# Adaptive-norm modulations: products on ScalarE, sums on GpSimd, in a two-block kernel on one core

## The chip, the core and the metric

One core of a Trainium2 chip runs the whole kernel. The core has five engines with queues of their own, each of which runs its instructions in order: TensorE (PE, its weight loads are shown as PEld), VectorE (DVE), ScalarE (ACT), GpSimd (POOL) and SyncE (SP). SP issues most DMAs, GpSimd some. Engines wait for one another by semaphores. The metric is the device time of one execution in microseconds (us). Before the change it is 1889.6 us, the median of 3 runs (1889.45 to 1890.53).

## What is computed

Two transformer-like blocks on a sequence of 512 tokens and width 1024, all in float32. The first mixes with RWKV-7 and mLSTM heads and has a mixture of 32 experts, the second mixes with a 31-tap convolution and Mamba-2 heads and has a dense feed-forward part. Each block modulates its norms and residuals with vectors that come from a condition `c`:

```
mod = jax.nn.silu(c) @ ada_w[l] + ada_b[l]
sh_m, sc_m, g_m, sh_f, sc_f, g_f = jnp.split(mod, 6, axis=-1)
h = modulate(rms_norm(x, mix_norm_w[l]), sh_m, sc_m)
...
x = x + g_m[:, None, :] * y
```

The second block has the same with two matrices of three parts each. So there are twelve vectors of 1024, each a product of a vector of 1024 with a 1024x1024 matrix (4 MB). Two of the twelve, the first block's shift and scale of its first norm, are made by a function of their own at the start; the change concerns the other ten.

## The kernel before

Weights come from HBM through SP as raw blocks of 128 partitions x 1024 floats (`wload`, L189, three raw buffers). `wcut` splits each: ScalarE copies a high part in TensorE's rounded format (`whi`, L201), VectorE subtracts it to get the low part (`wlo`, L203). There are two buffers of each. TensorE then does three matmuls per product (high times high, high times low, low times high). One such block is consumed in about 24 matmuls of 128x512.

The program is written as straight Python and ordered before it runs: a planner walks all instructions with priorities and modelled times and fixes the order of every engine's queue; the semaphore waits follow from the data. A tile's buffer is handed on when its last reader is done. Work that is not urgent is written as generators: `K.later(gen, q)` puts one into a list, `K.pump(n, q)` runs the next n of its steps, each at a priority that is lowered by `LATER[q]` (600 places for list 0), so that such a step fills gaps. `K.drain(q)` runs what is left.

A modulation is such a generator. `ada_acc` (L261 on) takes an accumulator `acc` of 128x1024 from the tag `v4` and loads the matrix in eight pieces `araw` of 128x1024 (512 KB, SP, L269), each in a buffer of `v4` as well. Partition p of piece q holds row 128q+p. VectorE multiplies the first piece by a column of silu(c) (L273) and for each of the other seven does one multiply-add into `acc` (L275). Then `ada_cols` (L281 on) sums over the partitions with eight matmuls against a column of ones (L289) and adds the bias (L290); `ada_row` (L299 on) does it with ones as weights (L311), adds the bias and stores the row to DRAM from GpSimd's queue (L317).

`v4` has five buffers in the first mixer, four in the second, five in the last part. The same tag serves others: in the first mixer `solve` (L627 on) holds three for A, T and Ttmp while it inverts triangular 32x32 blocks on VectorE, `halves` takes Dm (cleared on GpSimd, L664, filled by two transposes on VectorE, L666, read by TensorE for pX) and X (L674); `scan` takes two. In the second mixer the decays E use it.

Where the ten run: gate_m, scale_f and shift_f, gate_f, scale_m2 and shift_m2 are pumped in the first mixer, under `RWKV.project`, `MLSTM.project` and `scan`. The scan is a chain over 32 units in which TensorE, ScalarE (R1, SA, StP, s1) and VectorE (the state, masks, copies) alternate; beside it runs the mLSTM `mix` generator with four powers on GpSimd (L1086), each followed by scalings on ScalarE (L1088). gate_m2, scale_f2 and shift_f2 are pumped in the second mixer beside the out-projection of the SSM part (`ssm_out`, pso), the last of the 31-tap convolution on VectorE (`conv31`, co L1996) and its layer norm: `conv_sums` (mean by TensorE, L2025; differences L2029; squares on ScalarE L2034; sum L2037; a power on GpSimd L2017; `spread` by TensorE) and `conv_norm` (L2053, L2054). In the same stretch `conv_out` makes eight gates (sgc, a ScalarE activation that frees a PSUM tile, L2068). gate_f2 is pumped in the feed-forward part.

GpSimd computes little: fills, selects, the powers of rsqrt. Its queue also issues DMAs (spills, fetches, stores).

Of the kernel before, what the change touches and what calls it, by code (L numbers as in the profile page):

```python
# [11 lines left out]
AF = mybir.ActivationFunctionType  # L12
ALU = mybir.AluOpType
# [9 lines left out]
class Kern:  # L23
# [237 lines left out]
    def ada_acc(self, cs, w, n0, width=1024):  # L261

        nc = self.nc
        V = nc.vector
        acc = self.v4([128, 1024], name="acc") if width == 1024 else self.u(name="acc")
        nq = 1024 // width
        for q0 in range(0, 8, nq):
            raw = self.v4([128, nq, width], name="araw")
            nc.sync.dma_start(raw, w[q0 * 128:(q0 + nq) * 128, n0:n0 + width].rearrange("(q p) n -> p q n", p=128))  # L269
            for i in range(nq):  # L270
                q = q0 + i
                if q == 0:
                    V.tensor_scalar(acc, raw[:, i], cs[:, 0:1], None, op0=ALU.mult)  # L273
                else:
                    V.scalar_tensor_tensor(acc, raw[:, i], cs[:, q:q + 1], acc, op0=ALU.mult, op1=ALU.add)  # L275
            yield acc

        for _ in range(self.SLACK):
            yield acc
# [2216 lines left out]
```

## Time and profile before

| | |
|---|---|
| median of 3 runs | 1889.6 us |
| profiled execution, its own time | 1887.34 us |
| its span (first to last instruction) | 1885.6 us |
| TensorE busy | 1779.2 us (94%) |
| VectorE busy | 1369.6 us (73%) |
| ScalarE busy | 943.3 us (50%) |
| GpSimd busy | 137.0 us (7%) |
| mean granted TensorE clock | 0.978 |
| L275, the multiply-adds | 70, 89.7 us |

All durations of the trace are from the one profiled execution. A row of a group of instructions gives the line of the kernel, the engine, the operation, what it writes and reads by tile name, and the shapes. Busy time counts an instruction from its start to its end; two neighbours can overlap by some tens of nanoseconds. Idle time stands in brackets or at the end of a row, with what ended it, as far as the semaphores tell. The granted clock is a share of the full 2.4 GHz, averaged over the stretch; the lower level is 1.2 GHz.

### The profile page before, as it was taken

The numbers are of one execution on the slowest core, as the hardware profiler recorded it, in microseconds if no ns is written. First come the engines' busy times: TensorE is split into PE (matmuls) and PEld (weight loads), VectorE is DVE, ScalarE is ACT, GpSimd is POOL, SyncE is SP. The second block draws the span as 40 slices with busy tenths as digits, with TensorE's granted clock in tenths as the row PEclk, the third lists the DMA queues.
The fourth block names the chain that finished last, engine by engine and source line by source line (L and its number), as shares of the span: only waits on it lengthen the run. The fifth ranks groups of instructions, "written<-read, shape, count | busy, mean of one in ns | idle before, by whom it ended". The sixth has DMA issues, their size and how long they took to land. (4 is left out here: it accounts for less than half of the span.)

```text
span 1885.6 us, 27902 instructions
## 1 busy us (share of the span) xinstructions
PE 1779.2 (94%) x10696; PEld 1481.2 (79%) x10696; DVE 1369.6 (73%) x2166; ACT 943.3 (50%) x1568; POOL 137.0 (7%) x247
## 2 busy tenths in 40 slices
PE   6998989998999998699999999999999999999997
PEld 3675878887888887478887777878778988788997
DVE  4888877867899997678969999999766753333324
ACT  5732355455888887442348577552253632223223
POOL 4000020121000000220000000000000100000000
PEclk9998989998999998899999999999999999999999
DMA  8732555535899999854433243344834753333334
GB/s 287 255 103 76 150 171 176 177 135 179 275 354 351 360 363 317 283 73 125 123 90 101 79 124 95 96 133 134 230 94 151 237 183 90 101 101 90 118 108 150
DMA packets 332905, 322.27 MB, mean 171 GB/s; under 512 B 16813, under 2 KB 291791, under 8 KB 332764
## 3 DMA queue, kind: packets, MB, share of 16 engines
q1 hardware_dynamic: 319004, 281.96, 47.7%
q0 software_dynamic: 11520, 35.30, 6.4%
q10 hardware_dynamic: 2240, 3.15, 0.5%
q8 instruction: 86, 1.41, 0.3%
q14 instruction: 55, 0.45, 0.1%
HBM read 299.03 MB, written 21.33 MB: 170 GB/s over the span
## 5 line engine op out<-in xcount | busy, mean ns | idle before, releaser
L201 ACT ACTIVATE whi<-wraw 128x1024 fp32r<-128x1024 f32 (+1 forms) x281 | 293.5, 1045 | 618.9 <-PE pin L237 209.8
L203 DVE TENSOR_TENSOR wlo<-wraw,whi 128x1024 fp32r<-128x1024 f32 (+1 forms) x281 | 337.9, 1203 | 210.9 <-ACT whi L201 208.5
L236 PE MATMUL pin<-hhi,whi 128*128 128x512 f32 (+1 forms) x752 | 306.4, 407 | 10.7 <-ACT sgc L2068 4.9
L238 PE MATMUL pin<-hhi,wlo 128*128 128x512 f32 (+1 forms) x752 | 300.3, 400 | 1.7 <-DVE wlo L203 1.7
L237 PE MATMUL pin<-hlo,whi 128*128 128x512 f32 (+1 forms) x752 | 300.7, 400 | 0.0
L236 PEld LDWEIGHTS pin<-hhi,whi 128*128 128x128 f32 (+1 forms) x752 | 141.3, 188 | 49.5 <-ACT sgc L2068 5.7
L1996 DVE SCALAR_TENSOR_TENSOR co<-uc,cols,co 128x512 f32<-128x512 f32 x240 | 176.9, 746 | 2.7
L238 PEld LDWEIGHTS pin<-hhi,wlo 128*128 128x128 f32 (+1 forms) x752 | 141.2, 188 | 39.0 <-DVE wlo L203 2.6
L237 PEld LDWEIGHTS pin<-hlo,whi 128*128 128x128 f32 (+1 forms) x752 | 141.2, 188 | 35.8 <-issue 2.4
L203 DVE TENSOR_TENSOR mwlo<-mwraw,mwhi 128x1024 fp32r<-128x1024 f32 x129 | 154.2, 1214 | 13.5 <-ACT mwhi L201 12.9
L201 ACT ACTIVATE mwhi<-mwraw 128x1024 fp32r<-128x1024 f32 x129 | 133.2, 1050 | 19.6 <-PE pgu L1723 8.2
L238 PE MATMUL pff<-hhi,wlo 128*128 128x512 f32 x336 | 133.0, 396 | 0.3 <-DVE wlo L203 0.3
L236 PE MATMUL pff<-hhi,whi 128*128 128x512 f32 x336 | 133.0, 396 | 0.0
L237 PE MATMUL pff<-hlo,whi 128*128 128x512 f32 x336 | 132.9, 396 | 0.0
L275 DVE SCALAR_TENSOR_TENSOR acc<-araw,silu,acc 128x1024 f32<-128x1024 f32 x70 | 89.7, 1281 | 29.8 <-DMA araw<-in_w_ada_ffn_dram 15.4
L1723 PE MATMUL pgu<-mwhi,xs 128*128 128x256 f32 x392 | 99.9, 290 | 8.3 <-DVEq L1764 8.2
L453 PE MATMUL pres<-wlo,fhi 128*128 128x256 f32 x352 | 97.4, 277 | 1.5 <-DVE wlo L203 1.5
L452 PE MATMUL pres<-whi,flo 128*128 128x256 f32 x352 | 97.2, 276 | 0.0
L450 PE MATMUL pres<-whi,fhi 128*128 128x256 f32 x352 | 97.2, 276 | 0.0
L1724 PE MATMUL pgu<-mwlo,xs 128*128 128x256 f32 x392 | 97.0, 284 | 0.0
L1723 PEld LDWEIGHTS pgu<-mwhi,xs 128*128 128x128 f32 x392 | 75.5, 193 | 8.8 <-issue 8.3
L1724 PEld LDWEIGHTS pgu<-mwlo,xs 128*128 128x128 f32 x392 | 75.4, 192 | 0.7 <-DVE mwlo L203 0.3
(631 smaller groups left out, 3848.1 us busy)
## 6 DMA issues: line engine op xcount, KB each, us to landing
wraw<-in_w_in_dram SPq DMA_DIRECT2D x98, 512.0 KB, 3.8
mwraw<-in_moe_w_up_dram SPq DMA_DIRECT2D x61, 512.0 KB, 7.2
araw<-in_ada_w_dram SPq DMA_DIRECT2D x48, 512.0 KB, 8.1
wraw<-in_w_ffn_in_dram SPq DMA_DIRECT2D x44, 512.0 KB, 3.7
mwraw<-in_moe_w_down_dram SPq DMA_DIRECT2D x33, 512.0 KB, 6.2
mwraw<-in_moe_w_gate_dram SPq DMA_DIRECT2D x33, 512.0 KB, 7.5
wraw<-in_moe_w_down_dram SPq DMA_DIRECT2D x31, 512.0 KB, 6.1
wraw<-in_moe_w_gate_dram SPq DMA_DIRECT2D x29, 512.0 KB, 5.7
```

What stands on the lines that cost most here:

```text
L201: self.nc.scalar.activation(hi[:, :m], raw[:, :m], AF.Copy)
L203: self.nc.vector.tensor_tensor(lo[:, :m], raw[:, :m], hi[:, :m].bitcast(F32), op=ALU.subtract)
L236: t.matmul(out, lh, rh, start=start, stop=False)
L237: t.matmul(out, lh, rl, start=False, stop=False)
L238: return t.matmul(out, ll, rh, start=False, stop=stop)
L275: V.scalar_tensor_tensor(acc, raw[:, i], cs[:, q:q + 1], acc, op0=ALU.mult, op1=ALU.add)
L450: Te.matmul(o, yh[:, s], hi[:, k], start=(first and k == 0 and t == 0), stop=False, skip_group_check=True)
L452: Te.matmul(o, yl[:, s], hi[:, k], start=False, stop=False, skip_group_check=True)
L453: Te.matmul(o, yh[:, s], lo[:, k], start=False, stop=(last and k == kn - 1), skip_group_check=True)
L1723: Te.matmul(pg[:, j], x, hi[:, k], start=(kh == 0 and k == 0), stop=False)
L1724: Te.matmul(pg[:, j], x, lo[:, k], start=False, stop=(kh == 1 and k == 3))
L1996: V.scalar_tensor_tensor(c, u[:, j:j + 512], w(j), c, op0=ALU.mult, op1=ALU.add)
```

## The change

Inside `ada_acc` only. The first piece's scaling goes from VectorE to ScalarE. Each of the other seven multiply-adds becomes two instructions: ScalarE multiplies the piece in place by its column of silu(c), GpSimd adds it to `acc`. A piece's buffer is then free when GpSimd has added it. The loads, the sums over the partitions, the pumping and all priorities stay.

```diff
@@ ada_acc @@
             for i in range(nq):
                 q = q0 + i
+
                 if q == 0:
-                    V.tensor_scalar(acc, raw[:, i], cs[:, 0:1], None, op0=ALU.mult)
+                    nc.scalar.activation(acc, raw[:, i], AF.Copy, scale=cs[:, 0:1])
                 else:
-                    V.scalar_tensor_tensor(acc, raw[:, i], cs[:, q:q + 1], acc, op0=ALU.mult, op1=ALU.add)
+                    nc.scalar.activation(raw[:, i], raw[:, i], AF.Copy, scale=cs[:, q:q + 1])
+                    nc.gpsimd.tensor_tensor(acc, acc, raw[:, i], op=ALU.add)
             yield acc
```

## Rows read from the trace of the kernel before

**Rows 1.** busy time of each engine, from the page
```profile
PE 1779.2 (94%) x10696; PEld 1481.2 (79%) x10696; DVE 1369.6 (73%) x2166; ACT 943.3 (50%) x1568; POOL 137.0 (7%) x247
```

**Rows 2.** by stretch: length, busy (count) of PE PEld DVE ACT POOL, clock, DMA
```profile
47.00:115.00 68.00, 64.61 (x262) 47.17 (x261) 57.81 (x83) 46.12 (x59) 3.87 (x9) 1.00 0.66 212
115.00:250.00 135.00, 118.84 (x811) 93.81 (x809) 108.82 (x190) 43.35 (x70) 16.50 (x32) 0.94 0.41 119
250.00:375.00 125.00, 122.25 (x978) 107.23 (x978) 98.93 (x276) 64.59 (x201) 14.08 (x22) 0.97 0.55 173
1224.00:1336.00 112.00, 110.89 (x537) 89.76 (x533) 106.36 (x141) 40.88 (x61) 1.39 (x1) 1.00 0.50 147
1336.00:1398.00 62.00, 55.45 (x235) 43.15 (x235) 43.23 (x56) 27.39 (x39) 1.93 (x1) 0.94 0.56 162
```

**Rows 3.** changed lines: ns min/median/max; VectorE's waits (us, times); L275 by stretch
```profile
L273 DVE TENSOR_SCALAR acc<-araw,silu x10: 740/746/754, 47.3 to 1518.6; 128x1024 f32<-128x1024 f32 x10
...
L275 DVE SCALAR_TENSOR_TENSOR acc<-araw,silu,acc x70: 1256/1284/1286, 51.7 to 1537.4; 128x1024 f32<-128x1024 f32 x70
  DMA araw<-in_w_ada_ffn_dram: 15.4, 12
...
250.00:375.00 125.00, 26.95 (x21) 0.97 0.55 173
1224.00:1336.00 112.00, 13.77 (x11) 1.00 0.50 147
```

**Rows 4.** timeline of ScalarE in the out-projection: start us, us, idle before
```profile
1295.29 1.06 ACT L201 ACTIVATE whi<-wraw 128x1024 fp32r<-128x1024 f32 x1 [4.43 <-PE pso L237]
```

**Rows 5.** timeline around the convolution's mean, start us, us
```profile
1355.89 1.28 DVE L275 SCALAR_TENSOR_TENSOR acc<-araw,silu,acc 128x1024 f32<-128x1024 f32 x1 [2.91 <-DMA araw<-in_w_ada_ffn_dram]
...
1360.98 1.28 DVE L275 SCALAR_TENSOR_TENSOR acc<-araw,silu,acc 128x1024 f32<-128x1024 f32 x1 [2.67 <-DMA araw<-in_w_ada_ffn_dram]
...
1361.55 1.02 PE L2025 MATMUL pmean<-csum,mean 128*128 128x512 f32 x2
...
1362.61 1.23 DVE L203 TENSOR_TENSOR wlo<-wraw,whi 128x1024 fp32r<-128x1024 f32 x1 [0.34 <-ACT whi L201]
...
1363.75 2.48 DVE L2029 TENSOR_TENSOR co<-co,pmean 128x512 f32<-128x512 f32 x4
```

**Rows 6.** waits: who waited for whom, us in total, times, longest
```profile
PE pTT L692 <- DVE X L674: 8.2, 1, 8.2
...
PE pin L236 <- ACT sgc L2068: 4.9, 1, 4.9
...
PE spread L371 <- POOL rg L2017: 2.6, 2, 1.7
```

**Rows 7.** ScalarE's groups by shape: mean ns of one
```profile
L1831 ACT ACTIVATE yg<-yg,moe_cw 128x1024 f32<-128x1024 f32 x4 | 4.6, 1148 | 14.4 <-DMA yg<-ys,moe_idx 14.4
```

**Rows 8.** GpSimd: timeline of Dm's clear; group of a select (mean ns)
```profile
217.96 0.96 POOL L664 MEMSET Dm<- 128x1024 f32 x1 [48.19 <-DVE acc L275]
...
L139 POOL TENSOR_SCALAR_AFFINE_SELECT ident<-ones 128x128 f32<-128x128 f32 x1 | 0.3, 288 | 0.1
```

**Rows 9.** waits in the scan
```profile
ACT sq L1088 <- POOL ml_sm L1086: 3.9, 4, 1.1
```

**Rows 10.** timeline of two powers on GpSimd and VectorE beside the second
```profile
288.71 1.03 POOL L1086 TENSOR_TENSOR ml_sm<-ml_sm,mhalf 128x4 f32<-128x4 f32 x1 [8.22 <-DVE ml_sm L1085]
...
1043.60 1.23 DVE L203 TENSOR_TENSOR wlo<-wraw,whi 128x1024 fp32r<-128x1024 f32 x1
...
1043.76 1.95 POOL L2017 TENSOR_TENSOR rg<-rg,mhalf 128x4 f32<-128x4 f32 x1 [7.17 <-DVE rg L2016]
...
1044.74 2.32 DVE L1996 SCALAR_TENSOR_TENSOR co<-uc,cols,co 128x512 f32<-128x512 f32 x3
```

**Rows 11.** who reads and fills Dm: timeline of TensorE; durations ns min/median/max
```profile
236.48 1.58 PE L625 MATMUL pX<-Dm,AT 64*64 64x32 f32 x44
...
L666 DVE STREAM_TRANSPOSE Dm<-Tmat x2: 2146/2162/2177, 222.4 to 224.5; 32x1024 f32<-32x1024 f32 x2
```

## The prediction

> **What bounds the kernel now.** I read the page's busy line first, then the table of stretches, then the groups and waits of the changed line, and last single stretches of the timeline. TensorE is busy 94% of the span, VectorE 73%, ScalarE 50%, GpSimd 7% [rows 1]: whatever is taken off VectorE shortens the kernel only where TensorE stood idle for it. The ten modulations run in 47 to 375, 1224 to 1398 and around 1504 to 1540 us. There TensorE is 95 to 99% busy in three of the five stretches shown; in 1336 to 1398 it is busy 55.45 of 62 us, at a granted clock of 0.94 (part of it at 1.2 instead of 2.4 GHz) [rows 2]. So before any detail the gain has a ceiling: 6.6 us idle there, 2.8 us in the scan (250 to 375), 1.1 us in 1224 to 1336, 3.4 us in 47 to 115. Half of the 16 us idle in 115 to 250 is one wait of 8.2 us of the first join product for X [rows 6], with which no modulation has to do.
>
> **What is removed.** Ten scalings of 746 ns and 70 multiply-adds of 1284 ns [rows 3]: 7.5 + 89.9 = 97.4 us of VectorE. Nearly all of it lies beside matmuls. The weight blocks show how much cover there is: in the out-projection ScalarE makes a high part (1.06 us) after every 4.43 us of idle time, so a block lasts 5.49 us [rows 4]. High part and low part (1.23 us [rows 5]) take 2.3 us of it; 3.2 us of delay in either queue reach no matmul, since the copy is made one block ahead. VectorE's waits for a modulation's tile (15.4 us in 12 waits for the last matrix alone [rows 3], two of them 2.91 and 2.67 us [rows 5]) fit into these 3.2 us, and TensorE did not stop at them. One place does pay: the mean's matmuls end at 1361.55 + 1.02 = 1362.57, the subtraction that needs them starts at 1363.75, behind a low part that had itself been behind the late multiply-add of 1360.98 [rows 5]. That is 1.2 us. Behind it come the squares on ScalarE, behind these the gate's activation, and TensorE waits for the PSUM tile that this one reads (4.9 us [rows 6]).
>
> **What is added on ScalarE.** 80 products. Just such an instruction stands in the trace: a 128x1024 Copy with a scale per partition, 1148 ns [rows 7]; 80 x 1.148 = 91.8 us. In 250 to 375 there are 24 of them (21 multiply-adds [rows 3] and 3 scalings), 27.6 us on top of 64.6 of 125; in 1224 to 1336 13 (11 and 2), 14.9 us on top of 40.9 of 112 [rows 2]. ScalarE has the room. In 47 to 115 it is busy 46 of 68 us, and 17 products would bring it to 66: there they will be put later, up to the stretch from 115, where it has 43 of 135. What is new is what queues behind them: the high parts of the weights, the copies of the scan, the gates. The wait for the tile's landing moves along, from VectorE's queue to ScalarE's, and now stands in front of high and low part both.
>
> **What is added on GpSimd.** 70 additions of 128x1024. The trace has no such instruction. From below, a fill that only writes 128x1024 takes 0.96 us [rows 8]. A one-input select of 128x128 takes 288 ns [rows 8]; eight times that is 2.30 us, and twice this again, if two inputs take turns, 4.6 us. I take 2.3 us, since the select is the nearest row that reads, and its fixed part, counted eight times, makes room for the second input; the ends are 0.96 and 4.6. 70 x 2.3 = 161 us on an engine with 137 us of work: room too. The Trainium skill (GPSIMD Engine Reference, section 3.1 Elementwise) has 4497 ns for an addition of 2048 elements, by which an estimate for 1024 is 2.25 us; no run here shows it, and the sum would be the same.
>
> **Who is behind the additions.** On GpSimd's queue stand the small powers and the DMAs that it issues. Four powers in the mix (ScalarE waited 3.9 us for them [rows 9]) and two before a spread (TensorE waited 2.6 us for them [rows 6]) lie in the modulations' stretches. 21 additions x 2.3 = 48 us make GpSimd 39% busy in 250 to 375 and 28% in 1224 to 1398; a power that meets one waits 1.15 us on average: 4 x 0.39 x 1.15 + 2 x 0.28 x 1.15 = 2.4 us. At 0.96 us an addition it would be 0.5, at 4.6 us 8.
>
> **The two engines together.** A power takes 1.03 us beside small operations, and 1.95 us when a low part (two inputs in SBUF) began 0.16 us before it: it ended 0.88 us after that low part's 1044.83 [rows 10]. So GpSimd stands still while VectorE reads two inputs. Whether VectorE stands still for GpSimd the row hardly says: three convolution steps behind it took 2.32 us, 0.77 each [rows 10], and the power reads only four elements. The ends are 0 and the whole addition, 2.3 us for each of 70. I take 2.3 us where a low part meets one: alone that is inside the 3.2 us of cover, with a product in front of the high part it is 1.15 + 2.3 = 3.45, 0.24 over. With about 32 blocks and 24 pieces in 1224 to 1398 I let 8 blocks meet both: 1.9 us. The Trainium skill (SBUF — State Buffer, Who interferes with whom) says that it goes both ways: whichever starts first holds the shared read port for its whole instruction. The first half agrees with the 1.95 us; what the second half would make of the time is the lock rival below.
>
> **Longer life of a tile.** From one multiply-add to the next it is 5.09 us where a single buffer feeds the sum, 1.28 us of it the multiply-add [rows 5]. With product and addition in its place the step is 5.09 - 1.28 + 1.15 + 2.3 = 7.26 us, 2.2 more. SP's weight loads queue behind these issues, with three raw buffers in hand, so 2 us cost nothing there. In the solve, though, one of the five wide buffers goes from a modulation to Dm, cleared at 217.96 after a wait of 48 us for the last multiply-add [rows 8]. Six pieces x 2.2 = 13.0 us later is 231.0, plus 0.96 and two transposes of 2.16 [rows 11] is 236.3; TensorE reads Dm at 236.48 [rows 11]. It just fits: 0. Where an addition takes 4.6 us it is 14 us late.
>
> **The sum.** Long landing waits now ahead of the high part: 2.91 + 1.15 = 4.06, 0.85 over the cover; three like it, +2.6. Blocks that meet product and addition +1.9, powers +2.4. Gains: -1.2 for the subtraction, and -1.0 of the 2.8 us that TensorE idles in the scan, where VectorE goes from 98.9 to about 70 us while ScalarE goes to 92. Together +4.7 us on the profiled execution's 1887.3, which lies 2.3 us under the median of 1889.6: 1892.0 profiled, 1894.3 as a median. The case's own range is 1889 to 1900.
>
> **Rivals.**
> *The relief reaches TensorE (faster).* Without the late multiply-adds the squares come early, the gate's activation frees its PSUM tile, and the 4.9 us wait goes, with the clock: 0.94 over 62 us is 7.4 us at half speed, 3.7 us of work. 8.6 us less: 1881. For it: VectorE is the busiest helper, 95% in 1224 to 1336. Against it: the wait is for ScalarE's queue, and that gets longer.
> *The lock works against VectorE (slower).* Every addition stops the two-input steps of VectorE. In 1224 to 1336 VectorE's 106.4 us lose 15.3 (11 multiply-adds of 1.25, 2 scalings) and get 11 x 2.3 = 25.3: 116.4 in 112, 4.4 us too many, and what is late is the convolution's sum, on which the mean, the norm and the conv-out products hang. In 47 to 115 57.8 - 20 + 32 = 70 of 68, 2 too many. Two such stalls with a fall of the clock like that of 1336 to 1398 cost 3.7 each, 7.4, and Dm, with additions that wait for VectorE in turn, some 6 more: +20, 1910. It decides from the point where an addition in these stretches takes over 2 us of VectorE's time. For it: the 1.95 us power. Against it: VectorE has 26 us free in the scan and 19 us in 1336 to 1398 [rows 2], and the sum is not read before 1361.55 [rows 5], 25 us after that stretch.
> *All of it stays under the matmuls (no change).* 1889.6. For it: TensorE at 99% in the stretch where the pieces are densest, and the waits of 2.9 us that it did not feel. Against it: two in-order queues take part where one did.
>
> **How the numbers follow.** About 0.2% (3.8 us) is what a measurement of this kernel can tell from no change, so "same" is 1885.8 to 1893.4. The forecast gets 0.45, of which 0.17 falls inside that band and 0.28 above; the relief 0.25; the lock 0.15; no change 0.15. Faster 0.25, same 0.32, slower 0.43. The range runs from the relief's time, 1881, to just short of the lock's, 1908; the ends of the addition's cost (powers 0.5 to 8 us, Dm up to 14 late) lie inside it or in the tenth left out above.
>
> **What would show it.** Products of 1.15 us on ScalarE and additions near 2.3 us on GpSimd; low parts and convolution steps stretched to over 2 us would show the lock, an unchanged 1.23 and 0.75 us would refute it. ScalarE, not VectorE, waiting for the modulations' tiles; longer waits for the powers; Dm cleared near 231. The forecast is wrong if TensorE's idle time in 1336 to 1398 falls by more than 4 us, if the matmuls on a modulation's sum wait for GpSimd, or if the additions take 4 us.

## The result, and the profile after it

The changed kernel takes 1964.1 us (median of 4, 1962.85 to 1974.97) against 1890.1 for the kernel before: ratio 1.040, 95% interval 1.037 to 1.043. That is 74 us slower. The forecast was 4.7 us slower, and its range ended at 1908.

The page's busy line after the change, to be read against [rows 1]:

```profile
PE 1806.7 (92%) x10696; PEld 1496.1 (76%) x10696; DVE 1378.4 (70%) x2086; ACT 1020.6 (52%) x1646; POOL 316.8 (16%) x317
```

VectorE has 80 instructions less, 97.4 us by [rows 3], and yet it is busy 8.8 us more: its other steps became 106 us longer. TensorE does the same 10696 matmuls in 27.5 us more busy time, because the granted clock fell more often (0.964 of full speed on the mean, against 0.978), and is idle 49.4 us more (155.8 against 106.4). Together that is the 76.9 us by which the profiled execution grew.

The groups of the changed lines and of the steps that became longer (line, engine, operation, shapes, count | busy us, mean ns | idle before, and who ended it):

```profile
L1998 DVE SCALAR_TENSOR_TENSOR co<-uc,cols,co 128x512 f32<-128x512 f32 x240 | 205.1, 863 | 3.1
L277 POOL TENSOR_TENSOR acc<-acc,araw 128x1024 f32<-128x1024 f32 x70 | 181.0, 2586 | 254.2 <-ACT araw L276 225.9 <-issue 21.9 <-DMA araw<-in_w_ada_ffn_dram 4.8
L276 ACT ACTIVATE araw<-araw,silu 128x1024 f32<-128x1024 f32 x70 | 79.8, 1147 | 89.7 <-DMA araw<-in_w_ada_ffn_dram 57.1 <-DMA araw<-in_ada_w_dram 20.9 <-DMA araw<-in_w_ada_mix_dram 9.0
...
L730 DVE COPY x<-q 64x256 f32<-64x256 f32 x32 | 17.2, 537 | 0.8
L729 DVE COPY x<-q 64x256 f32<-64x256 f32 x32 | 15.7, 490 | 11.5 <-PE pq L762 11.2
```

The same three steps before the change:

```profile
L1996 DVE SCALAR_TENSOR_TENSOR co<-uc,cols,co 128x512 f32<-128x512 f32 x240 | 176.9, 746 | 2.7
L728 DVE COPY x<-q 64x256 f32<-64x256 f32 x32 | 9.3, 291 | 0.6
L727 DVE COPY x<-q 64x256 f32<-64x256 f32 x32 | 9.1, 284 | 3.2 <-PE pq L760 2.8
```

The convolution step went from a mean of 746 ns to 863; the scan's two copies went from 291 and 284 to 537 and 490. These are means over steps that are unchanged and a few that are very long. One place shows them singly. The timeline of VectorE at 102 us (start us, us), then GpSimd and TensorE in the same microseconds:

```profile
102.30 2.84 DVE L614 TENSOR_TENSOR q<-ur,P 128x512 f32<-128x512 f32 x1
105.06 2.83 DVE L615 SCALAR_TENSOR_TENSOR k<-ur,cols,k 128x512 f32<-128x512 f32 x1
107.81 2.83 DVE L594 SCALAR_TENSOR_TENSOR sq<-uk,cols,sq 128x512 f32<-128x512 f32 x1
```

```profile
101.14 8.95 POOL L277 TENSOR_TENSOR acc<-acc,araw 128x1024 f32<-128x1024 f32 x3 [2.44 <-ACT araw L276]
```

```profile
107.94 2.08 PE L617 MATMUL pbon<-k,rw_head 128*128 128x512 f32 x2 [7.10 <-DVE k L615]
```

Three additions run one behind the other, and three VectorE steps of some 0.7 us take 2.8 each: one step gets through per addition. TensorE needs the second of them and stands 7.1 us. The time in which a VectorE step is stopped counts as its duration, so the busy line shows a busy engine where there is a standing one.

Matching the matmuls of both traces one by one, TensorE is level with the kernel before until 94 us (on that kernel's clock), 12 us behind at 109, 25 at 230, 43 at 386, 42 still at 1246, 77 at 1340, and 77 at the end. So 43 us come from the first mixer and 35 from 1246 to 1340, where the last group of heads of the SSM part and its out-projection stand; the last of the ten modulations, in the final stage, costs nothing. That stretch before and after (length, busy PE PEld DVE ACT POOL, clock, DMA):

```profile
1246.00:1340.00 94.00, 92.89 (x426) 75.63 (x423) 88.75 (x116) 25.51 (x32) 1.39 (x1) 1.00 0.52 152
```

```profile
1288.00:1417.00 129.00, 105.01 (x426) 81.77 (x422) 113.81 (x106) 48.07 (x53) 57.16 (x21) 0.91 0.51 155
```

The same 426 matmuls: 12.1 us more busy at a clock of 0.91 instead of 1.00, 22.9 us more idle. Whom TensorE waited for there:

```profile
PE pso L238 <- DVE wlo L203: 16.4, 11, 3.6
PE pms L2012 <- DVE gsum L2262: 6.9, 1, 6.9
PE pso L236 <- ACT whi L201: 0.5, 1, 0.5
```

Low parts of weights and one sum of the SSM part, both VectorE's, make up 23.3 of its 24.0 us of idle time. ScalarE stands 49.6 us for the modulations' tiles in this part of the trace, in front of the high parts; that is the other suspect.

How the low parts come late can be read here. From 1310 to 1398 us VectorE is busy 87.22 of 88 us:

```profile
1310.00:1398.00 88.00, 72.88 (x281) 55.82 (x279) 87.22 (x82) 29.97 (x31) 37.76 (x14) 0.92 0.49 149
```

Twelve convolution steps and one low part of y are stopped in this stretch, and no low part of weights. But the low parts of weights stand behind them in VectorE's order: from 1330 on each starts 2.3 to 7.3 us after its high part is done, and takes its usual 1.2 us. Nine of TensorE's eleven waits for a low part, 12.4 of the 16.4 us, are for these nine. Only one wait (1.4 us) is for a low part that was stopped itself.

### The profile page after: what moved, and what is told of

The parts are those of the page before. It is cut to its first block, busy times and chain, and to the rows that moved or that the text cites. A ratio compares the mean times of both kernels' runs of the same rounds, so it can differ in the third digit from the quotient of the medians.

```text
span 1962.5 us, 28057 instructions
## 1 busy us (share of the span) xinstructions
PE 1806.7 (92%) x10696; PEld 1496.1 (76%) x10696; DVE 1378.4 (70%) x2086; ACT 1020.6 (52%) x1646; POOL 316.8 (16%) x317
## 5 line engine op out<-in xcount | busy, mean ns | idle before, releaser
L203 DVE TENSOR_TENSOR wlo<-wraw,whi 128x1024 fp32r<-128x1024 f32 (+1 forms) x281 | 349.7, 1245 | 253.9 <-ACT whi L201 245.9
L277 POOL TENSOR_TENSOR acc<-acc,araw 128x1024 f32<-128x1024 f32 x70 | 181.0, 2586 | 254.2 <-ACT araw L276 225.9
L1998 DVE SCALAR_TENSOR_TENSOR co<-uc,cols,co 128x512 f32<-128x512 f32 x240 | 205.1, 863 | 3.1
L276 ACT ACTIVATE araw<-araw,silu 128x1024 f32<-128x1024 f32 x70 | 79.8, 1147 | 89.7 <-DMA araw<-in_w_ada_ffn_dram 57.1
```

What stands on the lines that cost most here:

```text
L203: self.nc.vector.tensor_tensor(lo[:, :m], raw[:, :m], hi[:, :m].bitcast(F32), op=ALU.subtract)
L277: nc.gpsimd.tensor_tensor(acc, acc, raw[:, i], op=ALU.add)
L1998: V.scalar_tensor_tensor(c, u[:, j:j + 512], w(j), c, op0=ALU.mult, op1=ALU.add)
```

## The experiments

Two theories stood after the trace. **Lock:** an addition on GpSimd, which reads SBUF, stops VectorE's steps for its whole 2.4 us. **Queue:** ScalarE's product waits in order for a tile's landing, and the high parts and the scan's copies wait behind it. The first four runs take them apart. A ratio is always to the kernel before, from the same chip.

**Products on ScalarE, sums on VectorE.**

```
-                    nc.gpsimd.tensor_tensor(acc, acc, raw[:, i], op=ALU.add)
+                    V.tensor_tensor(acc, acc, raw[:, i], op=ALU.add)
```

> Products stay on ScalarE as in the change, the 70 sums go back to VectorE as plain additions, GpSimd gets nothing. Lock theory (an addition on GpSimd stops VectorE's two-input steps for its 2.4 us): nothing is left to stop them, 1888 to 1905 us, low parts and convolution steps back at 1.2 and 0.75 us. Queue theory (ScalarE's product waits in order for a tile's landing, and the weights' high parts and the scan's copies stand behind it): that queue is as in the change, so most of the 74 us stays, 1940 to 1965 us, and ScalarE's waits for the tiles are still some 90 us.

1897.2 us, ratio 1.0034 (1.0012 to 1.0055). The convolution step is at 746 ns again, and no VectorE step of a modulation's stretch is over 0.4 us longer than before. At 431 us TensorE is 4.6 us late, where the change had 43. So of 74 us all but some 6 go with the additions' engine. ScalarE's waits for the tiles are shorter than I wrote (67.0 us): its products wait less where the buffer comes back earlier.

**Products on VectorE, sums on GpSimd.**

```
-                    nc.scalar.activation(raw[:, i], raw[:, i], AF.Copy, scale=cs[:, q:q + 1])
+                    V.tensor_scalar(raw[:, i], raw[:, i], cs[:, q:q + 1], None, op0=ALU.mult)
```

> The other half alone: products as VectorE scalings in place (about 0.75 us each), the 70 sums on GpSimd as in the change, ScalarE gets nothing. Lock theory: the additions still stop VectorE, and VectorE has 70 x 0.75 = 52 us of scalings on top; 1935 to 1975 us, with convolution steps of over 2 us. Queue theory: ScalarE's queue is as before the change, so 1888 to 1905 us.

1960.1 us, ratio 1.036 (1.031 to 1.041), with ScalarE as before the change (942.4 us busy). The additions alone bring nearly the whole loss.

**The change for the four late modulations only.**

```
+                if not late:
+                    ...
+                        V.scalar_tensor_tensor(acc, raw[:, i], cs[:, q:q + 1], acc, op0=ALU.mult, op1=ALU.add)
...
+        for acc in self.ada_acc(cs, w, n0, late=name in ("gate_m2", "scale_f2", "shift_f2", "gate_f2")):
```

> The change for the four late modulations alone (the three beside the convolutions and the one in the last stage), the six early ones as before. By the two traces TensorE fell 35 us further behind between 1246 and 1340 us and nothing in the last stage: 1925 us (1918 to 1932) if the stages add up. If the delay of the late stage was only a consequence of how the early one had shifted its work: 1888 to 1900.

1927.7 us, ratio 1.020 (1.015 to 1.024): 37 us where I expected 35, so the stages add up. This kernel is the ground of most of what follows, since it leaves the first half alone.

**The same with fills in place of the additions, twice.**

```
-                    nc.gpsimd.tensor_tensor(acc, acc, raw[:, i], op=ALU.add)
+                    nc.gpsimd.memset(raw[:, i], 0.0)
+                    nc.gpsimd.memset(acc, 0.0)
+                    nc.gpsimd.memset(raw[:, i, 0:512], 0.0)
```

> As the kernel with the four late modulations changed, but each addition on GpSimd is three fills of 128x1024, 128x1024 and 128x512 (0.96 + 0.96 + 0.48 = 2.4 us), which only write; the sums are left out. ScalarE's queue, the length of the chain from landing to free buffer and GpSimd's occupation stay. Lock theory: a fill reads nothing and stops nobody, 1888 to 1900 us, convolution steps at 0.75 us. Queue theory: as with the additions, about 1925. A time in between gives each its share.

1891.0 us, ratio 0.9999 (0.998 to 1.002). In its trace, however, the two fills of the raw tile ran ahead of the third, and a piece took only 6.5 us. So the queue theory had not had its full chance, and a second control followed, with all three fills on the raw tile:

> A control of the run with fills: there the three fills came in another order and gave the raw buffer back after 1.5 us instead of 2.4, so that a piece took 6.5 us and not the 7.3 to 7.9 us of the additions. Here all three fills write the raw buffer (1024, 1024 and 512 elements, 2.4 us; sums left out for the four late modulations), so the buffer's round (3.7 us landing, 1.15 product, 2.4 fill) is 7.25 us, as with additions, and nothing reads. Pacing theory (ScalarE's order ties one weight block to one piece, so TensorE goes at 7.3 us a block instead of 5.5, about 16 blocks long): 25 to 33 us stay, 1915 to 1925. Lock theory: 1888 to 1898 us.

Ratio 1.0006 (0.9988 to 1.0024). ScalarE's waits in it from 1246 to 1420 us, and the convolution step beside fills that keep GpSimd as long as the additions did:

```profile
ACT araw L281 <- DMA araw<-in_w_ada_ffn_dram: 43.0, 12, 5.6
```

```profile
L2005 DVE SCALAR_TENSOR_TENSOR co<-uc,cols,co 128x512 f32<-128x512 f32 x240 | 177.6, 748 | 4.0 <-ACT co L2003 0.8
```

ScalarE stands nearly as long in front of the high parts as after the change (43 us, longest wait 5.6), and it costs nothing that can be measured (the interval ends at 4.5 us). What costs the 37 us of this stretch is that GpSimd reads SBUF. The queue theory falls as their cause.

**The stop by itself.** A kernel of nothing but groups of nine VectorE steps beside three instructions of GpSimd, for instance:

```
"two": (512, lambda o: V.tensor_tensor(o, e0, e1, op=ALU.subtract)),
...
"psum": (512, lambda o: V.tensor_tensor(o, pp, e1, op=ALU.mult)),
...
"add": lambda o: G.tensor_tensor(o, g0, g1, op=ALU.add),
```

Here V is VectorE and G is GpSimd. `e0` and `e1` are 128x512 in SBUF, `pp` is 128x512 in PSUM, `g0` and `g1` are 128x1024 in SBUF.

> None of the kernel's computation: only groups of nine VectorE steps on 128x512 (subtraction of two tiles in SBUF, convolution step, copy; a scaling of 128x1024; a product with one factor in PSUM, a copy from PSUM; a subtraction of 128x8), each group alone and beside three GpSimd additions of 128x1024, some also beside three fills or three copies on GpSimd. Lock theory, both ways: beside additions some steps with two SBUF inputs (the small one too) take about 2.4 us longer than alone, and the additions are longer than 2.4 us by a step or more; beside fills nothing changes. Open: the one-input copy and scaling of SBUF, the steps that read PSUM, and whether a one-input copy on GpSimd is enough to stop VectorE. Rival (they only share bandwidth): every step slows by a similar factor, fills included, and no step waits a whole addition.

The groups, named VectorE's step, V, and what ran on GpSimd beside it (busy us of the nine, mean ns):

```profile
L47 DVE SCALAR_TENSOR_TENSOR convVadd<-d,col,d 128x512 f32<-128x512 f32 x9 | 12.6, 1405 | 0.7 <-ACT d L76 0.5
L49 DVE TENSOR_SCALAR scalVadd<-d,col 128x1024 f32<-128x1024 f32 x9 | 12.6, 1400 | 0.5 <-ACT d L76 0.4
L46 DVE TENSOR_TENSOR twoVadd<-d,d 128x512 f32<-128x512 f32 x9 | 12.3, 1369 | 1.1 <-ACT d L76 0.8
L48 DVE COPY copyVadd<-d 128x512 f32<-128x512 f32 x9 | 9.9, 1104 | 0.7 <-ACT d L76 0.4
L46 DVE TENSOR_TENSOR twoVgcopy<-d,d 128x512 f32<-128x512 f32 x9 | 8.4, 930 | 0.6 <-ACT d L76 0.4
...
L46 DVE TENSOR_TENSOR twoValone<-d,d 128x512 f32<-128x512 f32 x9 | 6.2, 692 | 6.2 <-ACT d L39 5.9
L46 DVE TENSOR_TENSOR twoVfill<-d,d 128x512 f32<-128x512 f32 x9 | 6.2, 692 | 7.1 <-ACT d L76 6.8
...
L51 DVE COPY pcopyVadd<-pp 128x512 f32<-128x512 f32 x9 | 6.2, 689 | 0.2
L50 DVE TENSOR_TENSOR psumVadd<-pp,d 128x512 f32<-128x512 f32 x9 | 6.2, 686 | 0.1
...
L48 DVE COPY copyValone<-d 128x512 f32<-128x512 f32 x9 | 3.8, 427 | 1.0 <-ACT d L76 0.8
L52 DVE TENSOR_TENSOR smallVadd<-d,d 128x8 f32<-128x8 f32 x9 | 3.6, 399 | 9.0 <-ACT d L76 8.8
L52 DVE TENSOR_TENSOR smallValone<-d,d 128x8 f32<-128x8 f32 x9 | 1.5, 167 | 1.1 <-ACT d L76 0.8
```

Beside additions nine steps take 6.1 us longer than alone when both inputs are in SBUF (12.3 against 6.2), and so do one-input copies of SBUF (9.9 against 3.8). All of it falls on three of the nine, about 2.0 us each; the other six are as fast as alone, so the two engines do not share a rate. Steps with an input in PSUM keep their 0.69 us. Fills change nothing, but they lay beside the two-input groups only; beside one-input copies they are seen further below. A one-input copy on GpSimd is enough to stop VectorE (8.4 against 6.2). Even the subtraction of eight columns (0.167 us) once waited until an addition was over. The first additions of the group "two", and VectorE beside them:

```profile
49.99 7.83 POOL L55 TENSOR_TENSOR addWtwo<-g,g 128x1024 f32<-128x1024 f32 x3 [49.55 <-ACT g L76]
```

```profile
50.13 8.96 DVE L46 TENSOR_TENSOR twoVadd<-d,d 128x512 f32<-128x512 f32 x4 [0.84 <-ACT d L76]
```

Three additions and the steps beside them take turns, one for one. GpSimd loses little by it (7.83 us for three, 7.0 alone), VectorE an addition each time. The Trainium skill (SBUF — State Buffer, Who interferes with whom) says this of a step with two SBUF inputs: it meets a GpSimd instruction that reads SBUF, not one that only writes, and the second to come stands for the whole of the first. The subtraction's rows agree: 1369 ns beside additions, 930 beside copies, 692 beside fills and alone.

**Additions cut in four.**

```
+                    for s in range(4):
+                        f = slice(s * 256, s * 256 + 256)
+                        nc.gpsimd.tensor_tensor(acc[:, f], acc[:, f], raw[:, i, f], op=ALU.add)
```

> The change with every addition cut into four of 128x256 (about 0.65 us each; as much GpSimd time in sum or a little more). If what costs is VectorE's total time lost to additions: 1960 to 1990 us, as the change or slower. If it is that a single step on a chain waits for a whole addition (2.4 us) and now waits for a quarter at most: VectorE gets in between, single steps stretch by no more than 0.7 us, 1900 to 1930 us.

1992.8 us, ratio 1.053 (1.051 to 1.055): worse than whole additions, and a little above the first of the two ranges. The quarters in the groups:

```profile
L279 POOL TENSOR_TENSOR acc<-acc,araw 128x256 f32<-128x256 f32 x280 | 254.7, 941 | 237.4 <-ACT araw L276 208.0 <-issue 28.8 <-POOL acc L279 0.4
```

941 ns each on the mean, against 0.71 us for the shortest: 93 of the 280 take over 1 us. So GpSimd needs 254.7 us instead of 181.0, and the tiles come back later (ScalarE's wait for them rises from 89.7 to 140.4 us). VectorE is stopped more often, but each time for less: counting steps over 0.3 us longer than the same operation before, 117 for 70 us in sum, where whole additions stopped 53 for 97. The kernel is slower all the same, so the sum of the stops does not set the loss. Which of the two costs more, the later tiles or the number of stops, was not tried. Shorter instructions did not help.

**What the relief of VectorE is worth.** The fills for seven modulations, four late ones and three that run through the scan, which takes their sums off VectorE:

> As the kernel with fills in place of additions, for seven modulations: the four late ones, and the three that run from the solve through the scan (gate_f, scale_m2, shift_m2); sums left out for these. VectorE is relieved of 71 us and ScalarE has 56 products more. Lock theory: 1886 to 1896 us; what lies under 1890 is what the relief of VectorE is worth. Queue theory: the scan's 18 us of the change's delay are ScalarE's, 1900 to 1910 us.

Ratio 0.9988 (0.9973 to 1.0002). But these fills do stop something. GpSimd and VectorE in the scan of this run:

```profile
264.79 1.04 POOL L282 MEMSET araw<- 128x1024 f32 x1 [1.57 <-ACT araw L281]
```

```profile
264.64 0.29 DVE L736 COPY x<-q 64x256 f32<-64x256 f32 x1
264.96 1.01 DVE L737 COPY x<-q 64x256 f32<-64x256 f32 x1
```

The copy that begins during a fill takes 1.01 us instead of 0.29. Of the 64 such copies 22 take over 0.4 us, up to 1.08, and they lose some 10 us in sum; in the kernel before and in the two runs with late fills alone none takes over 0.36. So a fill spares VectorE's two-input steps, but not its copies from SBUF to SBUF. For the late four, where no VectorE step was longer beside fills, the relief is worth nothing that can be measured; in the scan the stopped copies could hide a small gain.

**How the stops reach TensorE.** VectorE is 94% busy in the late stretch before the change, so I asked whether it is simply overfull (its own 73.9 us and the 21 additions of the late-only kernel at 2.4 us make some 124, in 94) or whether single stops count. The convolution was cut, unchanged and changed:

```
+                if j <= 7:
                     V.scalar_tensor_tensor(c, u[:, j:j + 512], w(j), c, op0=ALU.mult, op1=ALU.add)
```

> The kernel before, with the convolution of 31 taps cut to 8 (23 of 30 steps per channel block left out): the ground for the next run. TensorE is 99% busy where these steps stand, so 1880 to 1892 us.

> The same cut of the convolution, with the four late modulations changed (products on ScalarE, sums on GpSimd). With all taps this change costs 37 us. If VectorE and GpSimd share one read port and the cost is that their work together (73 us of VectorE's own and 22 additions of 2.4 us, 126 us) has to pass where 94 us were to be had: without 23 of 30 taps VectorE's own is some 41 us, with 20 additions 89, and the difference to the kernel with few taps falls to 0 to 8 us. If it is that single low parts or sums on TensorE's chain are stopped by an addition wherever they meet one: these meet them as before, and 20 us or more stay. If ScalarE's order (high parts behind products) costs: 30 us or more stay.

1891.9 and 1920.4 us (ratios 1.000, 0.998 to 1.002, and 1.015, 1.013 to 1.017): 28.6 of 37 us stay. That does not make the overfull VectorE a small part, since the cut emptied only the second half of the stretch. The unchanged kernel with few taps:

```profile
1240.00:1290.00 50.00, 48.90 (x246) 39.05 (x245) 46.62 (x62) 20.58 (x34) 1.39 (x1) 1.00 0.57 172
1290.00:1340.00 50.00, 50.00 (x220) 41.04 (x219) 31.85 (x31) 10.13 (x10) 0.00 (x0) 1.00 0.81 233
```

In its first 50 us VectorE is as full as with all taps (46.62 us, 46.63 there). Matching the matmuls again, the changed kernel falls some 16 us behind it there and in the 20 us after, and 11 us from 1310 to 1340, where VectorE has room. These 11 us come another way. In the changed kernel with few taps, ScalarE, GpSimd and VectorE at 1341 us, each from its own timeline:

```profile
1341.52 1.15 ACT L281 ACTIVATE araw<-araw,silu 128x1024 f32<-128x1024 f32 x1 [5.30 <-DMA araw<-in_w_ada_ffn_dram]
1342.58 1.04 ACT L201 ACTIVATE whi<-wraw 128x1024 fp32r<-128x1024 f32 x1
1342.75 2.39 POOL L282 TENSOR_TENSOR acc<-acc,araw 128x1024 f32<-128x1024 f32 x1 [5.00 <-ACT araw L281]
1343.65 2.57 DVE L203 TENSOR_TENSOR wlo<-wraw,whi 128x1024 fp32r<-128x1024 f32 x1 [4.23 <-ACT whi L201]
```

The end of the product releases two things at once: the addition on GpSimd, and the high part behind it on ScalarE. The high part is done after 1.04 us, the addition after 2.39, so the low part, which needs the former, runs into the latter: 2.57 us instead of 1.22, and 2.57 to 2.64 in all seven rounds from 1320 us on. That is no chance meeting. With all taps it is rare: three low parts were stopped in the late stretch, two of them at its end. And a round takes 7.2 us (the next product starts at 1348.72), while TensorE could take a block every 5.5 [rows 4].

So I tried to break the round, with a fifth wide buffer (and 49 narrow ones instead of 50), changed and unchanged:

```
-    with K.stage("mix2", u2=50, v4=4):
+    with K.stage("mix2", u2=49, v4=5):
```

> The four late modulations changed, with five wide buffers instead of four in this stage (and 49 narrow ones instead of 50), so that a second raw tile can land while the first is worked on. Pacing theory: the round of a buffer no longer waits for the landing, 28 us or more of the 37 shrink to 5 to 20 us, 1896 to 1911. Lock theory: additions and the steps they stop are as many as before, 1920 to 1930 us.

> The kernel before with the same buffers, as the ground for the run with five buffers: 1886 to 1893 us by every theory, as a piece's 5.1 us were already under a block's 5.5.

1933.5 against 1896.0 us (ratios 1.022, 1.020 to 1.024, and 1.003, 1.001 to 1.004): 37.6, as with four buffers (both kernels came out a few us above the expected ranges). The pacing theory falls as a cause by itself. Last, both eased at once:

> Both eased: the convolution cut to 8 of 31 taps and five wide buffers, the four late modulations changed. If a full VectorE and the round of 7.3 us (landing, product, addition; one weight block behind each product) are each enough to keep the cost, the difference to the same kernel unchanged falls to 0 to 12 us. If single stops of low parts and sums on TensorE's chain cost wherever they fall, 20 us or more stay, as with few taps alone (29).

> Its ground: the kernel before with the same taps and buffers. 1890 to 1898 us by every theory, as few taps alone took 1891.9 and five buffers alone 1896.0.

1922.6 against 1896.4 us: 26.1 stay. On the clock of its ground, TensorE falls behind it by 24 us between 1264 and 1295 us and by 2.6 between 1295 and 1320; then the two run level. The steady round costs little here; what is left is one place, and the unchanged kernel has VectorE busy 51.1 of 55 us in it (1240 to 1295). GpSimd, VectorE and TensorE there, each from its own timeline:

```profile
1249.44 8.12 POOL L282 TENSOR_TENSOR acc<-acc,araw 128x1024 f32<-128x1024 f32 x3 [52.16 <-ACT araw L281]
1260.49 5.15 POOL L282 TENSOR_TENSOR acc<-acc,araw 128x1024 f32<-128x1024 f32 x2 [2.92 <-ACT araw L281]
```

```profile
1249.64 2.88 DVE L2004 SCALAR_TENSOR_TENSOR co<-uc,cols,co 128x512 f32<-128x512 f32 x1
1252.45 2.86 DVE L232 TENSOR_TENSOR ylo<-xbc,yhi 128x512 fp32r<-128x512 f32 x1
1255.24 2.88 DVE L2262 TENSOR_TENSOR xbc<-xbc,z 128x512 f32<-128x512 f32 x1
...
1261.51 1.93 DVE L2004 SCALAR_TENSOR_TENSOR co<-uc,cols,co 128x512 f32<-128x512 f32 x1
1263.36 2.69 DVE L2261 TENSOR_TENSOR xbc<-xbc,ea 128x384 f32<-128x384 f32 x1
```

```profile
1261.93 0.40 PE L237 MATMUL pso<-ylo,whi 128*128 128x512 f32 x1
1270.59 1.84 PE L2018 MATMUL pms<-ones,gsum 128*128 128x1 f32 x8 [8.26 <-DVE gsum L2268]
...
1272.86 0.63 PE L236 MATMUL pso<-yhi,whi 128*128 128x512 f32 x1
```

Five additions stop five VectorE steps in 16 us, four of them over 2 us longer and one 1.2: 9.8 us in sum. VectorE does not stand idle from 1246 to 1273 us, so all five delay what comes behind them in its order: the chain that ends the SSM part's last group (add, times z, square, sum, column sums, norm). TensorE waits 8.26 us for its sum, and then runs matmuls of 0.63 instead of 0.40 us at a granted clock of 0.62 over 1270 to 1280 us (part of it at 1.2 instead of 2.4 GHz). Behind that it waits 6.7 us more for low parts of weights and 4.1 for low parts of y.

## Why the prediction was wrong

**The step that failed** is "The two engines together". It priced the stop rightly, the whole addition, but let only 8 blocks meet it, "0.24 over" each: 1.9 us. Measured, the sums on GpSimd cost nearly all of the 74 us. Three assumptions of the step did not hold:

- *Only low parts were counted, as though the rest of VectorE's work had cover.* 53 steps were stopped, by 97 us in sum (steps over 0.3 us longer than the median of the same operation and shape before): 19.8 us in 47 to 125, 12.5 up to 270 with the solve, 21.2 in the scan, 39.5 late, 4.1 in the last stage. Eight of the 53 were low parts; 14 were convolution steps, in whose rear the low parts came late. By the trace those on chains of small steps cost TensorE at once: the products ahead of the 7.1 us wait, the solve's recurrence, the scan's copies, the SSM part's last sum. No slack of 3.2 us stands in front of these. That the one-input copies of the scan would be stopped too I had not considered.
- *Meetings were taken as chance.* The product releases the addition and the high part together; where VectorE has room, in the kernel with few taps, the low part came into the addition in every round. Where it has none, in the change itself, there was no need of a meeting: the whole queue was late.
- *I read the convolution steps behind the power, 0.77 us each [rows 10], as a sign that VectorE is hardly stopped.* The power overlaps the first of them by 0.97 us (it ends at 1045.71, they begin at 1044.74), but it reads four elements; the row could not show what a read of 1024 does.

**The lock rival** was the right mechanism, given 0.15 and +20 us. Its price was a budget of busy time by stretch, with 11 additions in 1224 to 1336. Three things were wrong with it. The additions moved: in the kernel before only 3 of the 24 late pieces ran ahead of 1309 us, because their multiply-adds stood behind convolution steps in VectorE's order; idle GpSimd takes them as they land, and 19 start in the 129 us that take the place of 1246 to 1340. With the 21 of the late-only kernel the same budget gives some 30 us too many for 1246 to 1340, near the 35 measured. It also missed what needs no full VectorE: in the kernel with few taps stopped low parts, in a slow round, cost 11 us where VectorE had room. And its two falls of the clock at 3.7 us each were 12.1 us in the late stretch alone, 27.5 in the whole run.

**Its other terms** mostly held. Products: 1148 ns forecast, 1147 measured. Addition: 2.3 forecast, 2.34 alone. Step per piece: 7.26 forecast, 7.2 measured in the kernel with few taps, where nothing else is late. Dm cleared near 231: 232.72, though the solve around it was late for other reasons. Powers: ScalarE waited 4.9 us for those of the mix instead of 3.9 [rows 9], 1.0 of the 2.4 forecast. The landing waits ahead of the high parts (+2.6) cost nothing measurable by the second control, though the longest there is 5.6 us; the 3.2 us of cover, by which the term was priced, is no limit that this run shows. The gains (-1.2 and -1.0) and the relief rival found no support: VectorE relieved of the four late modulations gave 0.9999 and 1.0006, of seven 0.9988, and the wait of 4.9 us for the gate's PSUM tile [rows 6] stands unchanged in the trace after.

**What stays open.** That the 43 us of the first half come from the stops follows from the kernel with sums on VectorE, 4.6 us late there; which of its stops costs how much was not tried. How much of the late 37 us is VectorE's full queue and how much is stopped steps on TensorE's chain is read from the traces alone; the cut of the convolution separates them only from 1310 us on. Of the 26 us that remain with both eased, the chain and the clock are read from the trace; moving the additions away from that chain was not tried.

## What to carry to other kernels

Before work is moved to GpSimd, ask what it reads, and what the VectorE steps beside it read. Here an instruction there that reads SBUF stopped the VectorE step that it met, if this had two SBUF inputs or copied SBUF to SBUF, for up to its whole length. A fill stopped the copies only, and steps that read PSUM were not stopped. Add the instruction's whole length to VectorE's time in the stretch where it will really run, which can be earlier than where the old work ran. Where that overfills VectorE, all that stands behind in its order comes late. Where it does not, list VectorE's small dependent steps, and ask whether one event releases both the GpSimd instruction and the VectorE step that follows. And look first whether relief of the engine would move the end at all; here kernels with the sums of four and of seven modulations left out were no faster.

## What the hardware showed beyond that

- A stop is inside the stopped step's duration: 0.69 us steps of 2.7 to 2.9, in a column that counts as busy. A step whose duration has two values, one an addition longer, gives it away; a group's mean (746 to 863 ns) hardly does.
- The two engines take turns one for one when both have work (three additions of 2.34, 2.67 and 2.67 us, and between them VectorE steps of 2.75, 2.71 and 2.71). Cutting the additions in four lowered the sum of VectorE's stops (97 to 70 us) but raised GpSimd's time by 41% (181.0 to 254.7 us), and cost 27 us more than whole additions.
- A step of 128x8, 0.167 us alone, waited for the addition like any other: one of the nine took 2.29 us.
- A fill on GpSimd, which reads nothing, stops VectorE's one-input copies from SBUF to SBUF: 0.29 us became up to 1.08.
